# Two rows per token fetched from DRAM in place of scatter products, for six of eight expert pairs

## The chip, the cores and the metric

One core of a Trainium2 chip runs the whole program. The time is the device time of one execution in microseconds; what is compared is the median of several runs. The core has five engines with instruction queues of their own: TensorE (PE in the profile, its weight loads PEld), VectorE (DVE), ScalarE (ACT), GpSimd (POOL) and SyncE (SP), and sixteen DMA engines that all queues share.

## The reference, cut to what matters

Two transformer blocks run on 256 tokens of 1024 features in float32. The change lies in the last stage of the second block, a mixture of experts with 4 groups of 4 experts, of which each token takes two:

```python
def _hier_moe(h, w_r1, b_r1, w_r2, b_r2, w_gate, w_up, w_down):
    hf = h.reshape(B * T, D)                       # 256 x 1024
    g_logits = (hf @ w_r1 + b_r1)
    g_sel = jnp.argmax(g_logits, axis=-1)          # one group of four
    ...
    top_p, top_i = lax.top_k(e_prob, EXPERT_TOPK)  # two experts of the group
    expert_id = g_sel[:, None] * EXPERTS_PER_GROUP + top_i
    combine = jnp.sum(jax.nn.one_hot(expert_id, N_EXPERTS) * (g_w * top_p)[..., None], axis=1)
    hid = jax.nn.silu(jnp.einsum('nd,edf->nef', hf, w_gate)) * jnp.einsum('nd,edf->nef', hf, w_up)
    hid = hid * combine[..., None]
    out = jnp.einsum('nef,efd->nd', hid, w_down)   # w_gate, w_up 1024 x 256, w_down 256 x 1024 per expert

# block 2: x = x + merged @ w_out, then x = x + _hier_moe(rmsnorm(x), ...)
```

## The kernel before, in words

**The stage.** `moe` (from L1388) computes the router and, for every token and expert, the token's place among the tokens of that expert (`place`; `sel` marks the chosen ones). `experts` (from L1505) does the rest. Each expert has 64 slots (`SLOTS`), and the sixteen experts are handled as eight pairs (`NP`), so a pair is one tile of 128 slots: expert 0 of the pair in partitions 0 to 63, expert 1 in 64 to 127. Should an expert have more than 64 tokens, a loop behind the stage repeats it for the rest; it then runs with `table=None`, by the old way in both kernels.

**A pair's steps**, in the order in which TensorE meets them:
- its tokens' rows, transposed: for pairs 0 to 2 (`NEAR`) by products with a one-hot matrix (`gather`), for pairs 3 to 7 by an indirect DMA on GpSimd's queue (`fetch`, L1566) and eight transposes (`turn_rows`, L1574);
- `up` (L1622): 32 matmuls with the weights of gate and up, into one PSUM bank;
- `act_up` (L1630, L1631): Silu with the router's factor on ScalarE, the product on VectorE;
- `turn` (L1637): two transposes of the hidden rows, copied by ScalarE into `hf` (L1639); VectorE builds `pb`, the one-hot matrix slots x tokens, from `spread`;
- `down` (L1656): 16 matmuls with w_down into two PSUM banks of 128 slots x 512; each is split into two parts of fewer bits (`split_act`, L320 on ScalarE and a subtraction on VectorE);
- `back` (L1670): eight matmuls of `pb` with these parts give each token its rows' sum, in four pieces of 128 tokens x 512 columns; VectorE adds each piece to `y` in SBUF. `base` is what the stage adds to; for pair 0 it stands in place of `y`.

**The order.** `then(f, ...)` makes the instructions of `f` follow the last entry of `chain`, the list of the last matmul of each step, so that TensorE's order is the one written in the loop: up(p), turn(p - 1), turn_rows(p + 1), back(p - 2), down(p - 1). Pairs 6 and 7 are not added by `back`; at the end `finish` collects their products in PSUM piece by piece, adds `y` and stores the output from ScalarE's queue.

**`spread`** holds, for every pair, the places of all tokens, the same in 64 partitions: ScalarE copies them to SBUF, GpSimd's queue writes them to DRAM (L1530) and reads them back with a broadcast (L1532).

**The weights.** A pair has six pieces of 1 MB (four of up, two of down), each loaded by two DMAs of 512 KB on SyncE's queue (`load_part`, L278). Thirteen buffers form a ring (`get_raw`, `load`), and the next piece's DMA is issued when TensorE has read the buffer that it takes. DMAs from SyncE's and ScalarE's queues share eight semaphore counters in turn, and each waits for the DMA that had its counter before it.

Of the kernel before, what the change touches and what calls it, by code (L numbers as in the profile page):

```python
# [6 lines left out]
BF16 = mybir.dt.bfloat16  # L7
F32 = mybir.dt.float32
# [21 lines left out]
PRE = (1, 1, 1, 1, 2, 0, 0, 0)  # L30
WAIT = (17, 8)
SLOTS = 64
NEAR = 3

OFF1 = dict(q=0, k=1024, v=2048, g=3072, li=4096, lg=5120, ga=6144, gb=7168)
OFF2 = {}
# [117 lines left out]
CST["cb0"] = (CST["cb1"][0] + 128, 128)  # L154

_o = CST["rc"][0]
for _n, _w in (("slot", SLOTS), ("upper", 16), ("limit", 40), ("row", 1), ("token", 2)):
    CST[_n] = (_o, _w)
    _o += _w
NCST2 = _o - CST["rc"][0]  # L160
# [2 lines left out]
def _consts():  # L163
    c = np.zeros((P, NCST), np.float32)

    def put(name, v):
        o, w = CST[name]
        c[:, o:o + w] = v

    put("ident", np.eye(P))  # L170
    put("ones", np.ones((P, 128)))
    inv = np.float32(10000.0) ** (-np.arange(0, 128, 2, dtype=np.float32) / np.float32(128))
    ang = (np.arange(T1, dtype=np.float32)[None, :] * inv.astype(np.float32)[:, None]).astype(np.float32)
    cos, sin = np.cos(ang.astype(np.float64)), np.sin(ang.astype(np.float64))
    put("rc", np.concatenate([cos, cos], 0))
    put("rs", np.concatenate([sin, -sin], 0))
    i = np.arange(P)
    put("tri", i[None, :] >= i[:, None])
    lg = np.log(1.0 - 2.0 ** (-5.0 - np.arange(8)))
    kd = np.zeros((P, 3, 8))  # L180
    kd[:META, 0] = np.exp(-np.arange(META)[:, None] * lg[None]) * 128 ** -0.5
    kd[:, 1] = np.exp(-(META + i)[:, None] * lg[None]) * 128 ** -0.5
    kd[:, 2] = np.exp(-(META + P + i)[:, None] * lg[None]) * 128 ** -0.5
    put("kdec", kd.reshape(P, 24))
    qd = np.zeros((P, 2, 8))
    for t in range(2):
# [7 lines left out]
    put("row", 1 + np.arange(P)[:, None] % SLOTS)  # L194
    put("token", P * np.arange(2)[None, :] + np.arange(P)[:, None] - 2 * SEQ)
# [16 lines left out]
class _Build:  # L212
# [1175 lines left out]
    def moe(self, xt, xs, logits, sums, root, eps, sq, transposed, keep):  # L1388
# [97 lines left out]
        y = self.experts(xt, None, xs, tabs, place, table, count)  # L1486
        n = self.most
        with self.tc.If(n > SLOTS):

# [12 lines left out]
    def store(self, queue, y, t, c):  # L1502
        queue.dma_start(self.a["out"][t * P:t * P + P, c], y[:, t, c])

    def experts(self, base, y, xs, tab, place, table=None, count=None):  # L1505

        nc, v, act, te = self.nc, self.nc.vector, self.nc.scalar, self.nc.tensor
        ident = self.c("ident")
# [1 line left out]
        pl = self.bigt(F32R, (P, 2, NEXP * SLOTS))  # L1510
        chain = []
        if table:
            spread = self.cp.tile([P, 2, NP, P], BF16, name="spread", tag="spread")

        def slots(h):
            near = 2 * NEAR
            for t, e, n in ((0, 0, 4), (0, 4, near - 4), (1, 0, near)) if h == 0 else ((0, near, NEXP - near), (1, near, NEXP - near)):
                last = v.tensor_tensor(
                    pl[:, t, e * SLOTS:(e + n) * SLOTS].rearrange("p (e s) -> p e s", s=SLOTS),
                    self.c("slot").unsqueeze(1).to_broadcast([P, n, SLOTS]),  # L1520
                    place[:, 16 * t + e:16 * t + e + n].unsqueeze(2).to_broadcast([P, n, SLOTS]), op=ALU.is_equal)
            return last

        def places_spread():

            pt, rows = self.sp(), self.t(P, BF16)
            te.transpose(pt[:, 0:P], self.placep, ident)
            act.copy(rows[0:32, :], pt[0:32, 0:P])
            store = self.dram.tile([2, 2, NP, P], BF16, name=self.name("dram"), tag="places")
            nc.gpsimd.dma_start(store.rearrange("j t p n -> t p j n"), rows[0:32, :])  # L1530
            for j in range(2):
                nc.gpsimd.dma_start(spread[j * SLOTS:j * SLOTS + SLOTS, :, :, :].rearrange("s t p n -> s (t p n)"),  # L1532
                                    store[j].rearrange("t p n -> (t p n)").unsqueeze(0).to_broadcast([SLOTS, 2 * NP * P]))


        xg = {}
# [21 lines left out]
                    act.mul(dst, ps[:, 0:n], self.p("gffn", k))  # L1558
            chain.append(mm)

        ids = self.keep(NP, I32)
        far = {}

        def fetch(p):
# [16 lines left out]
        if table:  # L1581
            with self.tc.issue_after(last.ins):
                table()
                slots(1)
        else:
            slots(1)
        cw, cr, cc = self.s(8, tag="cw"), self.s(8, tag="cr"), self.t(160)

        def places():
# [21 lines left out]
        hid, back_, outs = {}, {}, {}  # L1611

        def up(p, ps=None, parts=range(4)):

# [19 lines left out]
        def turn(p):  # L1634
            th, pt = hid.pop(p), self.sp()
            for b in range(2):
                mm = te.transpose(pt[:, b * P:b * P + P], th[:, b * P:b * P + P], ident)  # L1637
            hf, pb = self.t(SEQ), self.t(SEQ, F32R)
            act.copy(hf, pt[:, 0:SEQ])  # L1639
            if table:  # L1640
                v.tensor_scalar(pb.rearrange("p (t n) -> p t n", t=2), spread[:, :, p, :], self.c("row"), None, op0=ALU.is_equal)
            else:
                for t in range(2):
                    mm = te.transpose(pt[:, SEQ + t * P:SEQ + t * P + P], pl[:, t, p * P:p * P + P].bitcast(F32), ident)
                v.tensor_copy(pb, pt[:, SEQ:512])
            chain.append(mm)
            hid[p], back_[p] = hf, pb

        def down(p, ws, bs, pool=None):

            hf = hid[p]
            pd = [self.mm() for _ in bs]
            for k in range(2):
                for b, ps in zip(bs, pd):
                    for j, w in enumerate(ws[k]):
                        mm = te.matmul(ps[j * SLOTS:j * SLOTS + SLOTS, :],  # L1656
                                       hf[:, k * P + j * SLOTS:k * P + j * SLOTS + SLOTS],
                                       w[:, b * 512:b * 512 + 512], start=k == 0, stop=k == 1)
            chain.append(mm)
            for b, ps in zip(bs, pd):  # L1660
                oh, ol = pool[b] if pool else [self.t(512, F32R) for _ in range(2)]
                self.split_act(oh, ol, ps)
                outs.setdefault(p, {})[b] = oh, ol
# [36 lines left out]
        early = ExitStack()  # L1700
        then(gather, 0, NEAR)
        for p in range(NP):
            if p == 1:
                ps = then(up, p, None, range(3))
                then(turn, 0)
                then(up, p, ps, range(3, 4))
            else:
                ps = then(up, p)
            if p == 0:
                then(places)  # L1710
            act_up(p, ps)
# [19 lines left out]
            if p > 1:  # L1731
# [4 lines left out]
        then(turn, NP - 1)  # L1736
# [4 lines left out]
        for p, ws, pool in pairs:  # L1741
            then(down, p, ws, (0,), pool)
        then(down, *pairs[0][:2], (1,), pairs[0][2])
# [82 lines left out]
```

## Time and profile before

| | |
|---|---|
| time, median of 3 runs | 1015.45 us (1015.33 to 1015.57) |
| the profiled execution's own time | 1015.9 us |
| its span in the trace | 1014.0 us |
| mean granted TensorE clock | 0.998 |
| VectorE, ScalarE, GpSimd busy | 758.2 (75%), 578.9 (57%), 45.5 (4%) us |
| DMA over the span | 205.95 MB, mean 203 GB/s |
| the last slices of 25.35 us each, GB/s | 271, 351, 400, 410, 411, 99 |

The span reaches from the first to the last record of the trace; the execution's own time has 1.9 us more around it. The profile page divides the span into 40 slices, and the last row of the table shows how much the DMA engines moved in the last six of them. The expert stage takes the last 100 us or so, four of these slices.

### The profile page before, as it was taken

Reading aid. Unit: us, or ns where it says so; the run is one execution under the profiler, and the core shown is the slowest. Engines: PE = TensorE matmul, PEld = TensorE weight load, DVE = VectorE, ACT = ScalarE, POOL = GpSimd, SP = SyncE. Lnnn points to the kernel's source line nnn. Section 1 sums busy time; section 2 is a strip of 40 time slices with the busy share of each in tenths; the row PEclk is TensorE's granted clock in tenths of the full one; section 3 lists DMA queues with packets and bytes.
Section 4 is the critical chain, followed back from the end, with each engine's and each line's share of the span. In section 5 each row is a group of like instructions: output and inputs, shape, how many; then the busy total and the mean of one; then the engine's idle time right before and its main releaser. Section 6 shows DMA issues by size and latency. Waiting matters only on the chain.

```text
span 1014.0 us, 16390 instructions
## 1 busy us (share of the span) xinstructions
PE 1005.6 (99%) x6101; PEld 847.8 (84%) x6101; DVE 758.2 (75%) x1472; ACT 578.9 (57%) x1119; POOL 45.5 (4%) x68
## 2 busy tenths in 40 slices
PE   9999999999999999999999999999999999999997
PEld 8999998888888888888889888888888898963443
DVE  6898987788888787777798767988857688553443
ACT  6678546575567666555667556776656665431111
POOL 1500000000000000000001000000010100020000
PEclk9999999999999999999999999999999999999999
DMA  9745564447556556556534653455555637799992
GB/s 349 234 146 188 167 190 155 136 124 248 186 171 194 186 187 187 175 187 199 175 111 148 210 183 121 133 191 166 170 181 183 208 125 269 271 351 400 410 411 99
DMA packets 59238, 205.95 MB, mean 203 GB/s; under 512 B 6973, under 2 KB 9165, under 8 KB 59024
## 3 DMA queue, kind: packets, MB, share of 16 engines
q1 hardware_dynamic: 56512, 200.34, 58.9%
q0 software_dynamic: 1200, 2.84, 0.8%
q10 hardware_dynamic: 1440, 1.66, 0.5%
q8 instruction: 50, 0.82, 0.3%
q14 instruction: 36, 0.29, 0.1%
HBM read 204.07 MB, written 2.11 MB: 203 GB/s over the span
## 4 chain that ended last, share of the span: by engine, by line
PE 98%; DVE 0%; ACT 0%; issue 0%; DVEq 0%; ACTq 0%
PE mm L374 57%; PE mm L1622 5%; PE mm L366 4%; PE mm L368 4%; PE mm L367 4%; PE mm L1656 3%; PE mm L415 2%; PE mm L417 2%; PE mm L416 2%; PE sp L1670 1%; PE sp L437 1%; PE mm L560 1%; PE mm L1552 1%; PE mm L553 0%; PE sp L1574 0%; PE sp L401 0%
## 5 line engine op out<-in xcount | busy, mean ns | idle before, releaser
L374 PE MATMUL mm<-big,hi 128*128 128x512 f32 x1664 | 586.5, 399 | 0.0
L374 PE MATMUL mm<-big,lo 128*128 128x256 f32 x1664 | 435.5, 281 | 0.0
L289 DVE TENSOR_TENSOR lo<-raw,hi 128x1024 fp32r<-128x1024 f32 (+1 forms) x279 | 338.2, 1214 | 57.9 <-ACT hi L288 53.0
L374 PEld LDWEIGHTS mm<-big,hi 128*128 128x128 f32 x1664 | 303.8, 188 | 58.1 <-issue 0.7
L288 ACT ACTIVATE hi<-raw 128x1024 fp32r<-128x1024 f32 (+1 forms) x279 | 293.8, 1054 | 96.9 <-PE mm L374 29.3
L374 PEld LDWEIGHTS mm<-big,lo 128*128 128x128 f32 x1664 | 313.0, 188 | 15.0 <-ACT big L323 0.6
L386 ACT COPY tmp<-mm 128x256 f32<-128x256 f32 x194 | 71.4, 368 | 129.9 <-PE mm L374 129.7
L387 DVE TENSOR_TENSOR tmp<-mm,tmp 128x256 f32<-128x256 f32 x194 | 81.3, 420 | 56.3 <-ACT tmp L386 56.1
L366 PE MATMUL mm<-big,hi 128*128 128x256 f32 (+1 forms) x360 | 103.4, 287 | 0.0
L368 PE MATMUL mm<-big,lo 128*128 128x256 f32 (+1 forms) x360 | 102.4, 284 | 0.0
L367 PE MATMUL mm<-big,hi 128*128 128x256 f32 (+1 forms) x360 | 102.3, 284 | 0.0
L367 PEld LDWEIGHTS mm<-big,hi 128*128 128x128 f32 x360 | 67.9, 189 | 0.1
L366 PEld LDWEIGHTS mm<-big,hi 128*128 128x128 f32 x360 | 67.9, 189 | 0.0
L368 PEld LDWEIGHTS mm<-big,lo 128*128 128x128 f32 x360 | 67.8, 188 | 0.0
L431 POOL TENSOR_TENSOR sml<-sml,keep 128x2 f32<-128x2 f32 (+4 forms) x17 | 18.6, 1095 | 663.6 <-DVE sml L892 184.2
L1631 DVE SCALAR_TENSOR_TENSOR tmp<-mm,sml,tmp 128x256 f32<-128x256 f32 x8 | 3.9, 484 | 36.5 <-ACT tmp L1630 36.5
L415 PE MATMUL mm<-hi,big 128*128 128x512 f32 (+1 forms) x80 | 30.0, 376 | 0.0
L417 PE MATMUL mm<-lo,big 128*128 128x512 f32 (+1 forms) x80 | 29.8, 372 | 0.0
L416 PE MATMUL mm<-hi,big 128*128 128x512 f32 (+1 forms) x80 | 29.7, 371 | 0.0
L1622 PE MATMUL mm<-big,big 128*64 128x512 f32 x128 | 28.4, 594 | 0.0
L320 ACT ACTIVATE tmp<-mm 128x512 fp32r<-128x512 f32 x14 | 8.4, 597 | 31.5 <-PE mm L1656 31.5
L1630 ACT ACTIVATE tmp<-mm,sml 128x256 f32<-128x256 f32 x8 | 3.8, 474 | 39.1 <-PE mm L1622 39.1
(427 smaller groups left out, 1208.2 us busy)
## 6 DMA issues: line engine op xcount, KB each, us to landing
raw<-w SPq DMA_DIRECT2D x288, 512.0 KB, 4.0
big<-w SPq DMA_DIRECT2D x36, 512.0 KB, 10.0
exp<-w SPq DMA_DIRECT2D x36, 512.0 KB, 10.2
raw<-w SPq DMA_DIRECT2D x16, 448.0 KB, 3.3
big<-xT SPq DMA_DIRECT2D x4, 272.0 KB, 3.7
big<-xT SPq DMA_DIRECT2D x1, 1024.0 KB, 8.0
big<-memT SPq DMA_DIRECT2D x1, 1024.0 KB, 5.4
dram<-big POOLq DMA_DIRECT2D x2, 512.0 KB, 5.5
```

Of the source, the lines that this page charges most:

```text
L288: nc.scalar.activation(hi[:, :n], raw[:, :n], AF.Copy)
L289: low = nc.vector.tensor_tensor(lo[:, :n], raw[:, :n], hi[:, :n].bitcast(F32), op=ALU.subtract)
L366: nc.tensor.matmul(out, wh, xh[:, k, cols], start=first, stop=False)
L367: nc.tensor.matmul(out, wh, xl[:, k, cols], start=False, stop=False)
L368: nc.tensor.matmul(out, wl, xh[:, k, cols], start=False, stop=last)
L374: nc.tensor.matmul(*args, start=first and args is both, stop=last and args is both)
L386: nc.scalar.copy(ps, both[:, n:2 * n])
L387: nc.vector.tensor_tensor(ps, both[:, 0:n], ps, op=ALU.add)
L415: nc.tensor.matmul(ps[:, :w], xh[:, k, c], wh, start=k == 0, stop=False)
L416: nc.tensor.matmul(ps[:, :w], xl[:, k, c], wh, start=False, stop=False)
L417: nc.tensor.matmul(ps[:, :w], xh[:, k, c], wl, start=False, stop=k == last)
L1622: mm = te.matmul(ps[j * SLOTS:j * SLOTS + SLOTS, :], x(k)[:, j * SLOTS:j * SLOTS + SLOTS], w[:, kc * 512:kc * 512 + 512], start=k == 0, st ...
```

## The change

For pairs 0 to 5 (`THROUGH = 6`) the scatter products go. `down` of such a pair copies its two PSUM banks to SBUF by ScalarE and writes them to a DRAM tile `sums3` of 768 rows x 1024, from ScalarE's queue, two DMAs of 128 x 512 (256 KB) each. `wanted` works out for each token which rows of `sums3` are its own: of the first twelve experts the token's two, by slot number, as the largest value and the rest of the sum; a token that has fewer gets an index out of bounds, and its row stays as it was. It is seven small VectorE operations, with two new constants. Once the last of the sums is written, four indirect DMAs on GpSimd's queue fetch these rows into two buffers `got` that were set to zero, 128 tokens each, and VectorE adds them to `base` and `y`. `spread` and `pb` remain for pairs 6 and 7 only. The diff, cut:

```diff
+NEAR, THROUGH = 3, 6
...
-            spread = self.cp.tile([P, 2, NP, P], BF16, name="spread", tag="spread")
+            spread = self.cp.tile([P, NP - THROUGH, 2, P], BF16, name="spread", tag="spread")
...
-            nc.gpsimd.dma_start(store.rearrange("j t p n -> t p j n"), rows[0:32, :])
+            for t in range(2):
+                nc.gpsimd.dma_start(store[:, :, t, :].rearrange("j p n -> p j n"), rows[16 * t:16 * t + 16, :])
...
+        def wanted():
+            val, b, two = self.t(32), self.t(32), self.s(4, tag="two")
+            v.scalar_tensor_tensor(val, place, float(SLOTS), sel.bitcast(F32), op0=ALU.is_le, op1=ALU.mult)
+            v.tensor_tensor(b, place, self.c("base"), op=ALU.add)
+            v.tensor_tensor(val, val, b, op=ALU.mult)
+            val = val.rearrange("p (t e) -> p t e", t=2)[:, :, 0:2 * THROUGH]
+            v.tensor_reduce(two[:, 0:2], val, axis=AX.X, op=ALU.max)
+            v.tensor_reduce(two[:, 2:4], val, axis=AX.X, op=ALU.add)
+            v.tensor_tensor(two[:, 2:4], two[:, 2:4], two[:, 0:2], op=ALU.subtract)
+            v.tensor_scalar(wants, two, -1.0, None, op0=ALU.add)
...
+        # down
+            if table and p < THROUGH:
+                for b, ps in zip(bs, pd):
+                    orow = self.t(512)
+                    act.copy(orow, ps)
+                    nc.scalar.dma_start(self.sums3[p * P:p * P + P, b * 512:b * 512 + 512], orow)
+                return
...
         for p in range(NP):
-            if p == 1:
+            if p == 1 or table and p == NP - 1:
                 ps = then(up, p, None, range(3))
-                then(turn, 0)
+                then(turn, p - 1)
                 then(up, p, ps, range(3, 4))
...
-            act_up(p, ps)
+            if not 1 < p < NP - 1:
+                act_up(p, ps)
...
+            if 1 < p < NP - 1:
+                with self.tc.issue_after(held[0].ins):    # after turn's copy of hf
+                    act_up(p, ps)
...
-            if p > 1:
+            if p > 1 and not table:
                 then(back, p - 2, y)
             if 0 < p < NP - 1:
                 then(down, p - 1, weights(p - 1), (0, 1))
+            if table and p == THROUGH - 1:
+                got = [self.bigt(shape=(P, 2, D)) for _ in range(2)]
+                for g in got:
+                    nc.gpsimd.memset(g, 0.0)
+            if table and p == THROUGH:
+                for t in range(2):
+                    for i, g in enumerate(got):
+                        nc.gpsimd.indirect_dma_start(
+                            g[:, t, :], None, self.sums3[:, :],
+                            bass.IndirectOffsetOnAxis(wants[:, 2 * i + t:2 * i + t + 1].bitcast(mybir.dt.uint32), 0),
+                            bounds_check=THROUGH * P - 1, oob_is_err=False)
+                        v.tensor_tensor(y[:, t, :], g[:, t, :], (y if i else base)[:, t, :], op=ALU.add)
```

At the end the order becomes first half of down(6), turn(7), second half of down(6), first half of down(7), then `finish`, the second half of down(7), and `finish` again.

**Where TensorE's instructions stand: the end of pair 7's up.** Before, the last four matmuls of up(7) (line 1622), the transposes of pair 6's hidden rows, then the eight of `back` for pair 5 (1670), and the transposes of pair 7:

```order
L1622 MATMUL mm_10869<-big_10718,big_10285 64x512 x4
L1637 MATMUL sp_10889<-keep_91,tmp_10813 128x128 x2
L1670 MATMUL sp_10896<-tmp_10861,tmp_10820 128x512
L1670 MATMUL sp_10896<-tmp_10862,tmp_10820 128x512
L1670 MATMUL sp_10900<-tmp_10861,tmp_10820 128x512
L1670 MATMUL sp_10900<-tmp_10862,tmp_10820 128x512
L1670 MATMUL sp_10904<-tmp_10865,tmp_10820 128x512
L1670 MATMUL sp_10904<-tmp_10866,tmp_10820 128x512
L1670 MATMUL sp_10908<-tmp_10865,tmp_10820 128x512
L1670 MATMUL sp_10908<-tmp_10866,tmp_10820 128x512
L1637 MATMUL sp_10912<-keep_91,tmp_10886 128x128 x2
```

In the changed kernel (up 1642, turn 1657, down 1677):

```order
L1642 MATMUL mm_10804<-big_10664,big_10298 64x512 x4
L1657 MATMUL sp_10817<-keep_91,tmp_10757 128x128 x2
L1642 MATMUL mm_10804<-big_10671,big_10298 64x512 x4
L1677 MATMUL mm_10832<-big_10699,tmp_10820 64x512 x2
L1677 MATMUL mm_10832<-raw_10702,tmp_10820 64x512
L1677 MATMUL mm_10832<-raw_10704,tmp_10820 64x512
L1657 MATMUL sp_10841<-keep_91,tmp_10828 128x128 x2
```

The eight products are gone, pair 6 is turned ahead of the last quarter of up(7), and pair 7 behind the first half of down(6).

**Where ScalarE's instructions stand: around down(4).** Before: the Silu of one pair (line 1630), the copy of the turned hidden rows of the pair ahead of it (1639), and the first parts of the split of that pair's sums (320):

```order
L1630 ACTIVATE tmp_10725<-mm_10695,sml_10167 128x256
L1639 COPY tmp_10731<-sp_10728 128x256
L320 ACTIVATE tmp_10780<-mm_10770 128x512
L320 ACTIVATE tmp_10784<-mm_10771 128x512
L1630 ACTIVATE tmp_10813<-mm_10788,sml_10167 128x256
```

In the changed kernel (hidden rows' copy 1659, Silu 1650, sums' copies 1684, their stores 1685), with the counters that each waits for; DMAHW is one of the eight that the DMAs share:

```order
L1659 COPY tmp_10681<-sp_10678 128x256 [waits PE_49]
L1650 ACTIVATE tmp_10684<-mm_10648,sml_10179 128x256 [waits DMASW3_49,DMASW2_49]
L1684 COPY tmp_10716<-mm_10706 128x512 [waits DMAHW5_49,PE_49]
L1685 DMA dram_10177<-tmp_10716 128x512 [waits DMAHW0_49,Activation_49]
L1684 COPY tmp_10719<-mm_10707 128x512 [waits DMAHW7_49,PE_49]
L1685 DMA dram_10177<-tmp_10719 128x512 [waits DMAHW2_49,Activation_49]
L1659 COPY tmp_10754<-sp_10751 128x256 [waits PE_49]
```

The copy of the hidden rows now precedes the Silu, and each sum's copy is followed by a DMA issue that waits for a counter; the next pair's copy of hidden rows stands behind both.

## Rows read from the trace of the kernel before

**Rows 1.** Page, part 1: busy us (share of the span) x instructions, by engine.

```profile
PE 1005.6 (99%) x6101; PEld 847.8 (84%) x6101; DVE 758.2 (75%) x1472; ACT 578.9 (57%) x1119; POOL 45.5 (4%) x68
```

**Rows 2.** Chain of waits in order of time, 912 to 1014: start, length, work.

```profile
959.53 6.87 PE mm L1622 x32
966.39 0.37 PE sp L1637 x2
966.76 0.87 PE sp L1574 x8
967.64 1.85 PE sp L1670 x8
969.49 3.58 PE mm L1656 x16
973.07 6.87 PE mm L1622 x32
...
995.91 5.30 PE mm L1656 x24
1001.22 2.05 PE sp L1670 x8
1003.27 1.87 PE mm L1656 x8
1005.14 1.96 PE sp L1670 x10
```

**Rows 3.** Engines by stretch: length, busy (x) each, PEclk, DMA share, GB/s.

```profile
904.50:918.50 14.00, 14.00 (x74) 5.77 (x72) 1.98 (x7) 3.26 (x6) 3.15 (x4) 1.00 1.03 351
...
926.00:963.00 37.00, 37.00 (x184) 16.23 (x184) 17.13 (x30) 5.75 (x12) 2.97 (x3) 1.00 1.03 409
963.00:990.00 27.00, 27.00 (x134) 11.64 (x132) 11.42 (x20) 3.86 (x8) 0.00 (x0) 1.00 1.03 411
990.00:994.00 4.00, 4.00 (x22) 1.43 (x19) 0.00 (x0) 0.47 (x2) 0.00 (x0) 1.00 0.52 208
```

**Rows 4.** Last weight DMA: issue (timeline of SP); landing (DMA issues, 984.2 to 985).

```profile
984.26 0.33 SPq L278 DMA_DIRECT2D raw<-w  x1
...
raw<-w SPq DMA_DIRECT2D x1, 512.0 KB, 10.0
```

**Rows 5.** DMA queues and issues, 1003 to 1007, the first two output stores.

```profile
q10 hardware_dynamic: 288, 0.52, 35.5%
...
out<-big ACTq DMA_DIRECT2D x2, 256.0 KB, 2.1
```

**Rows 6.** DMA queues and issues, 926 to 963, three gathers of token rows.

```profile
q0 software_dynamic: 432, 0.72, 5.2%
...
big<-dram,keep POOLq DMA_INDIRECT x3, 7.5
```

**Rows 7.** DMA queues and issues, 895 to 899, token rows written beside weights.

```profile
DMA packets 450, 1.66 MB, mean 416 GB/s; under 512 B 47, under 2 KB 47, under 8 KB 449
...
q0 software_dynamic: 214, 0.82, 50.5%
...
big<-w SPq DMA_DIRECT2D x1, 512.0 KB, 3.8
```

**Rows 8.** DMA issues from 913.2 to 913.3, one weight DMA behind `spread`.

```profile
raw<-w SPq DMA_DIRECT2D x1, 512.0 KB, 5.2
```

**Rows 9.** Engines by stretch after the last matmuls, columns as in rows 3.

```profile
1007.30:1010.50 3.20, 0.02 (x1) 0.00 (x0) 1.18 (x3) 0.00 (x0) 0.00 (x0) 1.00 0.31 105
1010.50:1014.00 3.50, 0.00 (x0) 0.00 (x0) 0.00 (x0) 0.00 (x0) 0.00 (x0) 0.51 0.23 70
```

**Rows 10.** Groups by line, 918 to 995 (last row: whole span): busy, mean, idle.

```profile
L320 ACT ACTIVATE tmp<-mm 128x512 fp32r<-128x512 f32 x12 | 7.2, 597 | 28.9 <-PE mm L1656 28.9
...
L1639 ACT COPY tmp<-sp 128x256 f32<-128x256 f32 x6 | 2.2, 365 | 0.1
...
L289 DVE TENSOR_TENSOR lo<-raw,hi 128x1024 fp32r<-128x1024 f32 x263 | 320.8, 1222 | 51.8 <-ACT hi L288 46.8
```

More of the change, by code (lines that the diff above doesn't have):

```diff
@@ L32 @@
 SLOTS = 64
-NEAR = 3
+NEAR, THROUGH = 3, 6
 OFF1 = dict(q=0, k=1024, v=2048, g=3072, li=4096, lg=5120, ga=6144, gb=7168)
@@ L156 @@
 _o = CST["rc"][0]
-for _n, _w in (("slot", SLOTS), ("upper", 16), ("limit", 40), ("row", 1), ("token", 2)):
+for _n, _w in (("slot", SLOTS), ("upper", 16), ("limit", 40), ("row", 1), ("token", 2), ("base", 32), ("place", NEXP // 2)):
     CST[_n] = (_o, _w)
@@ L194, in _consts @@
     put("row", 1 + np.arange(P)[:, None] % SLOTS)
+    put("base", SLOTS * (np.arange(32) % NEXP)[None, :])
+    put("place", P * np.arange(NEXP // 2)[None, :] + np.arange(P)[:, None])
     put("token", P * np.arange(2)[None, :] + np.arange(P)[:, None] - 2 * SEQ)
@@ L1484, in table @@
             self.split_act(tabs[:, :, 0, :], tabs[:, :, 1, :], tab)
-        y = self.experts(xt, None, xs, tabs, place, table, count)
+        y = self.experts(xt, None, xs, tabs, place, table, count, sel)
         n = self.most
@@ L1503, in store, with experts @@
         queue.dma_start(self.a["out"][t * P:t * P + P, c], y[:, t, c])
-    def experts(self, base, y, xs, tab, place, table=None, count=None):
+    def experts(self, base, y, xs, tab, place, table=None, count=None, sel=None):
         nc, v, act, te = self.nc, self.nc.vector, self.nc.scalar, self.nc.tensor
@@ L1528, in places_spread @@
             act.copy(rows[0:32, :], pt[0:32, 0:P])
-            store = self.dram.tile([2, 2, NP, P], BF16, name=self.name("dram"), tag="places")
-            nc.gpsimd.dma_start(store.rearrange("j t p n -> t p j n"), rows[0:32, :])
+            store = self.dram.tile([2, NP, 2, P], BF16, name=self.name("dram"), tag="places")
+            for t in range(2):
+                nc.gpsimd.dma_start(store[:, :, t, :].rearrange("j p n -> p j n"), rows[16 * t:16 * t + 16, :])
             for j in range(2):
-                nc.gpsimd.dma_start(spread[j * SLOTS:j * SLOTS + SLOTS, :, :, :].rearrange("s t p n -> s (t p n)"),
-                                    store[j].rearrange("t p n -> (t p n)").unsqueeze(0).to_broadcast([SLOTS, 2 * NP * P]))
+                nc.gpsimd.dma_start(spread[j * SLOTS:j * SLOTS + SLOTS, :, :, :].rearrange("s p t n -> s (p t n)"),
+                                    store[j, THROUGH:NP].rearrange("p t n -> (p t n)").unsqueeze(0).to_broadcast([SLOTS, 2 * (NP - THROUGH) * P]))
         xg = {}
@@ L1559, in gather @@
             chain.append(mm)
-        ids = self.keep(NP, I32)
+        ids, wants = self.keep(NP, I32), self.keep(4, I32)
+        def wanted():
[8 more added lines that the diff above has]
+            v.tensor_scalar(wants, two, -1.0, None, op0=ALU.add)
         far = {}
@@ L1586, in experts @@
             slots(1)
+        if table:
+            wanted()
+            self.sums3 = self.dram.tile([THROUGH * P, D], F32, name=self.name("dram"), tag="sums")
         cw, cr, cc = self.s(8, tag="cw"), self.s(8, tag="cr"), self.t(160)
@@ L1609, in places @@
             v.tensor_tensor(cr, pw4[:, :, 0, 16], cc[:, 0:144].rearrange("p (a e) -> p a e", a=8)[:, :, 16], op=ALU.add)
-        hid, back_, outs = {}, {}, {}
+        hid, back_, outs, held = {}, {}, {}, {}
         def up(p, ps=None, parts=range(4)):
@@ L1638, in turn @@
             hf, pb = self.t(SEQ), self.t(SEQ, F32R)
-            act.copy(hf, pt[:, 0:SEQ])
+            held[0] = act.copy(hf, pt[:, 0:SEQ])
             if table:
-                v.tensor_scalar(pb.rearrange("p (t n) -> p t n", t=2), spread[:, :, p, :], self.c("row"), None, op0=ALU.is_equal)
+                if p >= THROUGH:
+                    v.tensor_scalar(pb.rearrange("p (t n) -> p t n", t=2), spread[:, p - THROUGH, :, :], self.c("row"), None, op0=ALU.is_equal)
             else:
@@ L1710, in experts @@
                 then(places)
-            act_up(p, ps)
+            if not 1 < p < NP - 1:
+                act_up(p, ps)
+            turned = p == 1 or table and p == NP - 1
             if p == 2 and y is None:
@@ L1718, in experts @@
                         early.enter_context(self.tc.issue_after(i.ins))
-            if p > 1:
+            if p and not turned:
                 then(turn, p - 1)
+            if 1 < p < NP - 1:
+                with self.tc.issue_after(held[0].ins):
+                    act_up(p, ps)
             if table:
@@ L1730, in experts @@
             early.close()
-            if p > 1:
+            if p > 1 and not table:
                 then(back, p - 2, y)
@@ L1734, in experts @@
                 then(down, p - 1, weights(p - 1), (0, 1))
-        then(turn, NP - 1)
+            if table and p == THROUGH - 1:
[10 more added lines that the diff above has]
+                        v.tensor_tensor(y[:, t, :], g[:, t, :], (y if i else base)[:, t, :], op=ALU.add)
+        if not table:
+            then(turn, NP - 1)
         last = self.bigt(F32R, (P, 4, 512))
@@ L1740, in experts @@
         first, second = [(NP - 2, 0), (NP - 2, 1)], [(NP - 1, 0), (NP - 1, 1)]
-        for p, ws, pool in pairs:
-            then(down, p, ws, (0,), pool)
-        then(down, *pairs[0][:2], (1,), pairs[0][2])
+        then(down, *pairs[0][:2], (0,), pairs[0][2])
+        if table:
+            then(turn, NP - 1)
+            then(down, *pairs[0][:2], (1,), pairs[0][2])
+        then(down, *pairs[1][:2], (0,), pairs[1][2])
+        if not table:
+            then(down, *pairs[0][:2], (1,), pairs[0][2])
         finish(y, self.PIECES[:2], first + second)
```

## The prediction

> **What bounds the kernel now.** I read four views in this order. The page's busy table first: TensorE works 1005.6 us of a span of 1014.0 [rows 1], so at first sight whatever leaves TensorE leaves the time. Then the chain of waits in order of time, over the expert stage [rows 2]. A pair of experts costs 13.54 us there, from 959.53 to 973.07: up 6.87, turn 0.37, the turned rows of a later pair 0.87, back 1.85, down 3.58, and no idle piece stands between them. Third, the busy time of every engine by stretch [rows 3], for the column that the first two views do not have: from 926 to 990 the DMA engines show a share of 1.03 (over 1, since their records overlap a little) at 409 to 411 GB/s, and they fall quiet only after 990. This is a second resource with no room. A weight DMA of 512 KB takes 0.524 MB / 0.410 = 1.28 us of it, so the twelve of a pair take 15.3 us, 1.8 more than TensorE needs for a pair: the stage lives on a lead that was fetched earlier and shrinks. Fourth, the last weight DMA by itself: issued at 984.26, landed 10.0 us later [rows 4], that is at 994.3. Its first reader is the 13th of the 24 matmuls that begin at 995.91 [rows 2], at 995.91 + 12 x 0.221 = 998.6. What is left of the lead at the end is 4.3 us.
>
> **The change part by part.** *Removed from TensorE:* `back` of pairs 0 to 5, eight matmuls each, six pieces of 1.85 us in the chain [rows 2]: 6 x 1.85 = 11.1 us, all on today's path. If the weights were always there, the span would be 1014.0 - 11.1 = 1002.9.
>
> *Moved on TensorE and ScalarE:* without `back`, hf of a pair must be ready after the 0.87 us of turned rows alone. It is now copied before the Silu; the copy takes 0.365 [rows 10] and fits, and pair 6, which has no turned rows behind it, is turned inside up(7) with a quarter of it (1.72 us) as cover. Cost 0. If that cover were short, down would start a few tenths late. *ScalarE and VectorE:* the two copies out of PSUM per pair cost ScalarE what its half of the split cost, 0.597 each [rows 10]; the two DMA issues per pair stand behind them in its queue, and ScalarE is busy 5.75 of 37 us [rows 3]. VectorE loses four adds and two subtractions per pair. The eight small operations of `wanted` and `places_spread`'s second DMA fall where VectorE is busy 1.98 of 14 us [rows 3]. All at 0. Each store also shares one of eight counters with weight DMAs and waits for the one that had it before; ScalarE then holds the next hf. I take 0, because that weight was issued several DMAs earlier and TensorE will be waiting for later weights anyway; the other end is a few us of waiting on ScalarE that the same DMA wait covers.
>
> *Added to the DMA engines,* the part that decides. Every byte that moves before the last weight delays it, since there is no idle share between 926 and 990.
> - Twelve stores of 256 KB (128 rows of 2 KB). The nearest row is the output stores, the same shape on the same queue: two of them take 35.5% of 4.0 us = 1.42 us of all sixteen engines [rows 5], twelve 8.5, and 8.3 after dividing by the 1.03. Lower end 3.15 MB at 409 GB/s = 7.7, upper 8.5. All twelve precede the last weight: the last leaves between 977.4 (where down(5) ends now, 973.07 + 13.54 = 986.6, less 5 x 1.85) and 986.6. That loads and stores share one rate is seen where the token rows are written to DRAM beside weights: half the share each, 416 GB/s for both together [rows 7].
> - Four gathers. The reference's own routing sends 388 of 512 (token, expert) choices to the first twelve experts, so 388 rows of 4 KB, 1.59 MB. Three fetches of the same kind moved 0.72 MB in 5.2% of 37 us = 1.92 us [rows 6]; 1.59 MB takes 4.25, and 4.1 after the 1.03. Lower end 3.9 (409 GB/s). They start once the last store has landed (2.1 us after its issue [rows 5]) and land some 7.5 us after theirs [rows 6], also before the last weight.
> - `spread` shrinks from 512 to 128 KB. In the stretch of the old one, 904.5 to 918.5, the engines moved 351 GB/s instead of 409 [rows 3]: 14.0 - 4.91/0.409 = 2.0 us lost, and with its own 1.3 us it cost 3.3; three quarters are 2.5. But the weight DMA behind it is issued only at 913.2 to 913.3, when TensorE frees its buffer, and lands 5.2 us later [rows 8]; a lone one needs 3.8 [rows 7]. So at most 1.4 comes forward. I take -1.4, with 0 and -2.5 as ends.
>
> *The sum.* The last weight lands at 994.3 + 8.3 + 4.1 - 1.4 = 1005.3. TensorE alone could read it by about 988, so DMA sets the end. Behind the landing come two matmuls of down(7) 0.44, the first product pieces 2.1, the second half of down(7) 1.87, the last pieces 1.96, and what now follows the last matmul, 1014.0 - 1007.1 = 6.9 [rows 2]: 13.3 us. Span 1018.6, 4.6 more than now. The profiled execution took 1015.9 for its span of 1014.0, so I expect 1020.5 for such a one; it lies 0.45 above the median of 1015.45, hence **1020.0** as the time. The ends of the terms give 9.1 to 12.8 instead of 11.0, so 1018.1 to 1021.9. The change loses if it puts more than 1014.0 - 13.3 - 994.3 = 6.4 us before the last weight. Where the stall goes: the lead of 4.3 turns into some 18 us of waiting in sum (11.1 that TensorE comes earlier and 11.0 that the weights come later), from pair 5 or 6 on. The four VectorE adds (1.222 each [rows 10]) end before the last split needs VectorE.
>
> The Trainium skill, "DMA: Bandwidth & Descriptors", section Specifications, puts the fabric's ceiling for the sixteen engines at 435 GB/s; by it the stores would be an estimated 7.2 us and the sum 1.1 us less. The trace stays at 409 to 416, so the rows' price stands.
>
> **The rivals.**
> (a) *Stores ride along.* Stores read SBUF and weights write it; if an engine moves one while it moves the other, the twelve cost the weights nothing. Then 4.1 - 1.4 = 2.7 us are added, below the 6.4 that decide, and the span is 994.3 + 2.7 + 13.3 = 1010.3: 3.7 faster, 1011.7. Against it: the halved shares in [rows 7]. For it: that row is a stretch of 4 us, and for half of it no weights were queued. This is the other side, and the point is stores at under 3.7 us. Chance 0.11.
> (b) *TensorE stays the bound*, as the busy table suggests, with weights arriving in time all the same: 1015.45 - 11.1 + 0.3 = 1004.6. It needs the engines to carry more than 411 GB/s, which no stretch after 926 shows. Chance 0.04.
> (c) *The clock falls.* TensorE would work about two thirds of the time from pair 6 on. After its last matmul at 1007.3 the granted clock is still 1.00 until 1010.5 and then 0.51, the lower level of 1.2 GHz [rows 9]; before that it never waited in this stage, so the trace does not say what short waits do. If the 6.4 us of matmuls behind the last weight ran at the lower level throughout, 6.4 more: 1026.4; for half of them, 1023.2, which I take. Chance 0.14. The Trainium skill, "TensorE: Matmul & The Clock Gate", section HAM oscillation, tells of a kernel whose matmuls came in bursts between DMA waits and began each at the low clock; by that rule (c) is the case.
> (d) *Smaller on every term*, or weights that regain part of it in a bubble of today's stream (the 351 GB/s stretch): 6.4 to 8.4 us added, no difference that can be told, about 1016. Chance 0.09.
>
> **How the numbers follow.** The forecast, weights late by 9 to 13 us and the clock held, has 0.62. A difference of 0.2% (2.0 us) is about what a measurement of this kernel can tell from none. Faster is (a) and (b): 0.15. Same, 1013.4 to 1017.5, is (d): 0.09. Slower is the forecast and (c): 0.76. The range takes in the forecast's own 1018.1 to 1021.9, (d), and most of (c): 1013.5 to 1025.0; it leaves out (a), (b) and the worst of (c), 0.19 together.
>
> **What would show it.** Right: up to about pair 4 a pair takes 11.7 us on TensorE without waits; from pair 5 or 6 on, idle time before the matmuls of up and down, ended by weight DMAs; the DMA share 1.0 until past 1003 and the last weight landing near 1005; 13 us from there to the end. The stores' queue should show about 0.7 us of all engines per store. Wrong: a last weight before 1000 (a), no waits on TensorE (b), a granted clock under 1.0 before the last matmul (c), or waits of TensorE that end on ScalarE or VectorE, which I have put at nothing.

## The result, and the profile after

| | before | after |
|---|---|---|
| time, median of 6 runs each | 1015.53 us (1015.33 to 1019.02) | 1023.57 us (1022.27 to 1025.91) |
| ratio after to before | | 1.0076, 95% interval 1.0056 to 1.0095 |
| the profiled execution's own time, its span | 1015.9, 1014.0 us | 1023.4, 1021.6 us |
| mean granted TensorE clock | 0.998 | 0.998 |

The change makes the kernel 8 us slower; 4.6 were forecast, and the time lies inside the range of 1013.5 to 1025.0. Two of the six runs (1025.82 and 1025.91) had a mean clock of 0.996 and 0.995 and were 2.1 to 3.6 us longer than the other four; they have no trace, so where in the program their clock fell is open.

In this document L is the time from the first matmul of down(0) to the last packet of the weights' DMA queue, worked out from each profile's records; it leaves out where the expert stage begins. L was 78.5 us before and is 90.3 now. (The expectations of e1 to e4 count it by the chain, from 916.81 to the landing at 1007.33, which gives 90.5 and 78.8, some 0.25 more; the later ones count it as here.)

The busy table of the page, which answers to [rows 1], looks as if nothing had happened, though 48 matmul records of 0.23 us are gone:

```profile
PE 1006.0 (98%) x6053; PEld 841.3 (82%) x6053; DVE 740.0 (72%) x1441; ACT 578.8 (57%) x1119; POOL 53.6 (5%) x75
```

The chain of waits in order of time (start, length, work) is the view that shows it. Up, turned hidden rows, turned rows, down now stand as L1642, L1657, L1591, L1677, the products of `finish` as L1697:

```profile
916.81 3.43 PE mm L1677 x16
...
931.94 6.87 PE mm L1642 x32
938.81 0.37 PE sp L1657 x2
939.18 0.87 PE sp L1591 x8
940.05 3.58 PE mm L1677 x16
943.64 6.87 PE mm L1642 x32
...
966.85 6.08 DMA dram<-tmp
...
973.41 7.67 DMA exp<-w
...
981.10 8.25 DMA big<-w
...
993.93 13.40 DMA raw<-w
...
1007.38 1.07 PE mm L1677 x2
1008.45 2.14 PE sp L1697 x8
1010.59 1.87 PE mm L1677 x8
1012.46 1.96 PE sp L1697 x10
```

A pair takes 943.64 - 931.94 = 11.70 us without a wait, 1.84 less than in [rows 2]; that part of the plan works. From 966 on the chain runs through DMAs: one store of sums, then weights to the last one, which lands at 1007.33. The engines by stretch (columns as in [rows 3]) show why they are late:

```profile
926.00:945.00 19.00, 19.00 (x98) 7.43 (x96) 3.36 (x6) 3.83 (x8) 1.98 (x2) 1.00 1.03 416
...
985.00:990.00 5.00, 4.02 (x16) 1.12 (x15) 0.00 (x0) 0.00 (x0) 0.00 (x0) 1.00 1.02 404
990.00:995.00 5.00, 4.91 (x18) 1.20 (x14) 0.03 (x1) 0.85 (x2) 1.98 (x2) 1.00 0.93 330
995.00:1000.00 5.00, 3.59 (x10) 0.85 (x12) 0.46 (x1) 0.33 (x1) 1.98 (x2) 1.00 1.01 394
1000.00:1005.00 5.00, 3.79 (x12) 0.88 (x12) 3.05 (x3) 1.12 (x3) 0.00 (x0) 1.00 1.02 411
1005.00:1010.00 5.00, 3.69 (x11) 1.57 (x12) 4.01 (x5) 0.60 (x1) 0.00 (x0) 1.00 0.19 76
```

The DMA share stays near 1 until 1005, ten to fifteen us longer than before, at 394 to 416 GB/s; the granted clock stays at 1.00 throughout. One stretch, 990 to 995, has a share of 0.93 and carries only 330 GB/s.

TensorE's waits from 963 on, as the profile lists them (us in total, times, longest), add up to 5.8:

```profile
PE mm L1677 <- DMA raw<-w: 3.9, 5, 1.2
PE mm L1642 <- DMA big<-w: 1.0, 2, 0.8
PE mm L1642 <- DMA exp<-w: 0.9, 2, 0.7
```

TensorE's last piece ends 7.3 later than before (1014.42 against 1007.10). Take off 1.3 for a later start of the stage and add the 11.1 that were removed: 17.1 us of waiting. By this sum the other 11.3 sit inside busy time. TensorE's timeline (start, busy, group, idle before it) shows where:

```profile
997.26 1.07 PE L1677 MATMUL mm<-raw,tmp 128*64 128x512 f32 x2 [1.17 <-DMA raw<-w]
...
999.93 1.08 PE L1677 MATMUL mm<-big,tmp 128*64 128x512 f32 x4
```

A matmul of down stands in the trace as two records. Two records, the matmul of one expert, take 1.07 us; four, the matmuls of both experts of a pair, take 1.08: they have 64 columns each and run side by side, their records beginning within 0.01 us of each other. When the second expert's weights land a DMA later than the first's, they run one after the other, and TensorE counts as busy all the while.

### The profile page after: what moved, and what is told of

Same layout as the page of the kernel before. It is cut to its first block, busy times and chain, and to the rows that moved or that the text cites. A ratio compares the mean times of both kernels' runs of the same rounds, so it can differ in the third digit from the quotient of the medians.

```text
span 1021.6 us, 16313 instructions
## 1 busy us (share of the span) xinstructions
PE 1006.0 (98%) x6053; PEld 841.3 (82%) x6053; DVE 740.0 (72%) x1441; ACT 578.8 (57%) x1119; POOL 53.6 (5%) x75
## 4 chain that ended last, share of the span: by engine, by line
PE 93%; DMA 4%; DVE 1%; ACT 0%; issue 0%; SPq 0%; DVEq 0%; ACTq 0%
PE mm L377 57%; PE mm L369 4%; PE mm L371 4%; PE mm L370 4%; PE mm L1642 4%; PE mm L1677 2%; DMA raw<-w 2%; PE mm L418 2%; PE mm L420 2%; PE mm L419 2%; PE sp L440 1%; DMA big<-w 1%; DMA exp<-w 1%; DMA dram<-tmp 1%; PE mm L1556 1%; PE sp L404 0%
## 5 line engine op out<-in xcount | busy, mean ns | idle before, releaser
L1592 DVE TENSOR_TENSOR big<-sp,keep 128x512 f32<-128x512 f32 x10 | 6.9, 686 | 54.2 <-PE sp L1591 54.2
L1642 PE MATMUL mm<-big,big 128*64 128x512 f32 x128 | 31.3, 597 | 1.0 <-DMA big<-w 1.0
L1659 ACT COPY tmp<-sp 128x256 f32<-128x256 f32 x8 | 3.0, 372 | 47.8 <-PE sp L1657 47.8
L419 PE MATMUL mm<-hi,big 128*128 128x512 f32 (+1 forms) x80 | 29.7, 372 | 0.0
L1642 PE MATMUL mm<-exp,big 128*64 128x512 f32 x96 | 25.4, 597 | 1.1 <-DMA exp<-w 0.9
```

The source lines that it names most:

```text
L419: nc.tensor.matmul(ps[:, :w], xl[:, k, c], wh, start=False, stop=False)
L1642: mm = te.matmul(ps[j * SLOTS:j * SLOTS + SLOTS, :], x(k)[:, j * SLOTS:j * SLOTS + SLOTS], w[:, kc * 512:kc * 512 + 512], start=k == 0, st ...
```

## The experiments

The time of each is a median beside runs of before on the same chip; the ratio is to those. These medians of before lie between 1015.5 and 1016.4 us, so two times of the table can differ by up to 0.9 for that alone.

| run | time, us | ratio to before, 95% interval | L, us |
|---|---|---|---|
| before | 1015.5 | | 78.5 |
| the change | 1023.6 | 1.0076 (1.0056 to 1.0095) | 90.3 |
| e1 stores from GpSimd's queue | 1022.9 | 1.0060 (1.0042 to 1.0078) | 89.9 |
| e2 half width | 1021.6 | 1.0039 (1.0022 to 1.0055) | 88.9 |
| e9 half width, GpSimd's queue | 1016.7 | 1.0010 (1.0001 to 1.0019) | 85.0 |
| e3 no fetch | 1019.4 | 1.0026 (1.0014 to 1.0037) | 86.9 |
| e4 no stores, no fetch | 1011.1 | 0.9936 (0.9919 to 0.9953) | 78.5 |
| e5 before, without back | 1011.8 | 0.9958 (0.9943 to 0.9973) | 78.0 |
| e6 before, with stores | 1022.2 | 1.0060 (1.0044 to 1.0075) | 88.1 |
| e7 two pairs through DRAM | 1022.8 | 1.0066 (1.0052 to 1.0080) | 83.1 |
| e10 the same, adds late | 1019.8 | 1.0046 (1.0030 to 1.0062) | 82.6 |
| e11 one pair, adds late | 1021.1 | 1.0056 (1.0037 to 1.0075) | 80.9 |
| e12 one pair, adds in between | 1016.6 | 1.0011 (1.0002 to 1.0020) | 80.7 |
| e13 two pairs, adds in between | 1016.0 | 0.9998 (0.9989 to 1.0007) | 83.4 |

### The bytes: e3, e4, e5, e6

e3 leaves out the fetch, e4 the stores as well:

```diff
-                        nc.gpsimd.indirect_dma_start(g[:, t, :], None, self.sums3[:, :], ...)
...
-                    nc.scalar.dma_start(self.sums3[p * P:p * P + P, b * 512:b * 512 + 512], orow)
```

> The four indirect fetches of sums are left out (the two buffers stay zero, so the result lacks the sums of pairs 0 to 5); the stores stay. Theory (bytes): the last weight lands 4.1 us earlier (86.4 after down(0) begins) and the time falls by 4. Rival 1 (shared counters): the fetches are not on these counters; nothing changes before them, and the last weight comes under 1 us earlier. Rival 3 (fetches land beside or behind the last weights, since they are issued at 992.6 to 996.5 and the last weight at 993.9): 1 to 2 us.

> Stores and fetches both left out (result lacks the sums of pairs 0 to 5); ScalarE's copies, the smaller spread and the new order stay. Theory (bytes): the last weight lands about 12.4 us earlier (78.1 after down(0) begins; 78.8 before the change), and the time falls by 12 to about 1011, still later than TensorE alone would need (1004 to 1006), because the weights themselves are what DMA has no room for. Rival 4 (TensorE bound once the added transfers go): 1004 to 1006.

L fell by 3.4 without the fetch (4.1 expected), and by another 8.3 without the stores; then it is what it was before the change, to 0.1, and the time is 12.5 below the changed kernel's (13.4 if each is taken against its own runs of before), where the theory had 12. TensorE is not the bound even then: 1011.1 is 6.5 above the 1004.6 that it would need by the forecast.

e4 also answers for `spread`, whose smaller size is still in it: nothing came of it. In the stretch of [rows 3] in which the old one was read, e4 shows

```profile
904.50:918.50 14.00, 14.00 (x74) 5.65 (x72) 1.68 (x7) 2.88 (x5) 3.21 (x4) 1.00 0.97 341
```

341 GB/s for 351. The DMA share is 0.97 there instead of 1.03, so the engines now carry less: argued, not tried, the weights already issued come sooner and the next have to wait until TensorE frees a buffer.

e5 takes only the products away from the kernel before, e6 only adds twelve stores to it:

```diff
-            if p > 1:
+            if p > 1 and not table:
                 then(back, p - 2, y)
+            elif p == 2:
+                v.tensor_copy(y, base)
```

> The kernel before with the scatter products and adds of pairs 0 to 5 left out (their sums are missing from the result), nothing added. Theory (the weights' own stream has no room): the last weight still lands 78.5 us after down(0) begins, so of the 11.1 us that leave TensorE only the lead of 4.3 and little more is gained: 4 to 5 us less than before, 1010.5 to 1011.5. Rival 4 (TensorE bound, the DMA engines follow): 11 less, 1004.5.

```diff
                 outs.setdefault(p, {})[b] = oh, ol
+                if table and p < 6:
+                    nc.scalar.dma_start(self.sums3[p * P:p * P + P, b * 512:b * 512 + 512], oh.bitcast(F32))
```

> The kernel before with twelve added stores of 256 KB from ScalarE's queue (the first part of each split of pairs 0 to 5, to a DRAM tile that nobody reads), nothing removed. Theory (bytes): the last weight lands 8.3 us later, 86.9 after down(0) begins; the lead of 4.3 is used up, and the time grows by 4 (8.3 - 4.3). Rival (stores ride along with loads on other paths): 78.5 still, and no change of time.

e5 gained 4.2 us of the 11.1 taken away, with L within 0.5 of before: the weights are the floor, and the busy table's 99% was not the whole bound. e6 lost 6.3 where 4 were expected: L grew by 9.5, not 8.3, with stretches such as

```profile
996.00:1002.00 6.00, 4.65 (x14) 1.19 (x13) 2.34 (x5) 0.97 (x2) 0.00 (x0) 1.00 0.91 341
```

so that something besides bytes holds weights up where stores stand among them. SyncE's queue, which issues the weights, waited 26.1 us for the stores in e6, and by itself e6 cannot tell bytes from such waits. Stores that ride along with loads would have left L alone here and, with the waits gone, in e1 below; there L is 89.9, and that rival is out.

### The counters: e1, e2, e9

In the changed kernel SyncE's queue, which issues the weights, waited for the stores, by its list of waits from 925 to 1005 (us in total, times, longest):

```profile
SPq L281 <- DMA dram<-tmp: 26.0, 10, 5.7
```

A weight DMA waits for the DMA that had its counter before it, eight back in the joint order of both queues; where that is a store, the weight cannot be issued before down has run, been copied, stored and landed. SyncE's queue waited before the change as well, 40.7 us in the same stretch for other weights; so the 26.0 us are not a loss by themselves, and it takes a run to price them.

```diff
-                    nc.scalar.dma_start(self.sums3[...], orow)
+                    nc.gpsimd.dma_start(self.sums3[...], orow)
```

> The twelve stores of sums are issued from GpSimd's queue instead of ScalarE's, so they no longer share the eight counters with the weight DMAs; bytes and everything else as in the changed kernel. Theory (bytes on DMA engines that have no room): the last weight lands 90.5 us after down(0) begins, as in the changed kernel (1007.33 - 916.81), within 1 us, and the time stays within 1 us of it. Rival 1 (weight DMAs held back on the shared counters: SyncE's queue waited 26.0 us for stores): the last weight comes 2 us or more earlier, up to 8, and the time falls by as much. Rival 2 (ScalarE held up by its store issues): TensorE's waits on ScalarE go, under 1 us.

The wait is gone, and L hardly moves (89.9 for 90.3). The dip is filled, as the stretch 970 to 1000 shows, first of the changed kernel, then of e1:

```profile
970.00:1000.00 30.00, 26.57 (x94) 8.15 (x92) 2.42 (x5) 3.00 (x7) 3.96 (x4) 1.00 1.01 394
```

```profile
970.00:1000.00 30.00, 26.75 (x94) 8.28 (x92) 2.92 (x6) 3.30 (x8) 8.72 (x8) 1.00 1.03 411
```

The bytes alone then hold L nearly where it was.

e2 halves the width of sums and fetched rows, with the stores on ScalarE's queue; e9 is e2 with the edit of e1:

```diff
-            self.sums3 = self.dram.tile([THROUGH * P, D], F32, ...)
+            self.sums3 = self.dram.tile([THROUGH * P, D // 2], F32, ...)
...
-                    nc.scalar.dma_start(self.sums3[p * P:p * P + P, b * 512:b * 512 + 512], orow)
+                    nc.scalar.dma_start(self.sums3[p * P:p * P + P, b * 256:b * 256 + 256], orow[:, 0:256])
...
-                            g[:, t, :], None, self.sums3[:, :],
+                            g[:, t, 0:D // 2], None, self.sums3[:, :],
```

> The sums are stored and fetched at half width: the twelve stores have 128 KB instead of 256, the four fetches rows of 2 KB instead of 4, the number of DMAs and their order stay; half of each token's sums is left out of the result. Theory (bytes): half of the stores' 8.3 and of the gathers' 4.1 us go, the last weight lands 6.2 us earlier (84.3 after down(0) begins), and the time falls by 6. Rival 1 (shared counters): a store still has to be issued and to land before the weight DMA that has its counter; it lands perhaps 1 us sooner, and the time falls by under 2.

> Half-width stores and fetches as in the run before (half of each token's sums is left out of the result), with the stores issued from GpSimd's queue, so that they share no counter with the weights. Theory now (both bounds stand beside each other: bytes, and the store-to-weight wait, which took over when only the bytes were halved): with both eased the DMA engines stay at 400 to 410 GB/s until the last weight, which lands 33.4 MB / 0.400 = 83.5 to 84.5 us after down(0) begins instead of 88.9, and the time falls 5 to 6 us below the changed kernel's. Rival (neither bytes nor counters: TensorE's own order of reading holds the last buffers): 88 to 89 again, and 1 to 2 us.

e2 came out as the rival had it: L fell by 1.4, not 6.2, and SyncE's queue waited 29.7 us for the stores. e9 settles it: with the counters apart as well, no wait for a store is left, L falls by 5.3 (to 85.0, where 83.5 to 84.5 were expected) and the time by 6.9. The stretch 955 to 990, first of e2, then of e9:

```profile
955.00:990.00 35.00, 32.50 (x140) 11.23 (x136) 3.62 (x7) 4.43 (x9) 1.80 (x1) 1.00 0.97 370
```

```profile
955.00:990.00 35.00, 33.49 (x149) 12.26 (x146) 3.62 (x7) 4.62 (x10) 8.69 (x10) 1.00 1.03 411
```

370 GB/s with the counters shared, 411 without. As far as these runs tell, two bounds stand within 1.4 us of each other in the changed kernel, bytes first and the store-to-weight wait right behind; relieving one alone shows little.

### Fewer pairs: e7, e10 to e13

With the lead of 4.3 us, one or two pairs through DRAM should pay. All five have back for the remaining pairs:

```diff
-NEAR, THROUGH = 3, 6
+NEAR, THROUGH = 3, 2
...
-            if p > 1 and not table:
+            if p > 1 and (not table or p - 2 >= THROUGH):
                 then(back, p - 2, y)
```

> The changed kernel with pairs 0 and 1 through DRAM only and pairs 2 to 7 by products (THROUGH = 2, back for pairs 2 to 5). Theory: TensorE saves 2 x 1.85 = 3.7; four stores cost 2.6 to 2.8 and the fetch of 136 rows (0.56 MB) 1.4, so the last weight lands 82.5 to 82.8 after down(0) begins, and with the changed kernel's 14.3 behind it the span is 915.4 + 82.7 + 14.3 = 1012.4, 1 to 2 us below before. Rival 1 (stores held against weights by the counters throughout): the same as before or slower.

L came close to the expected 82.5 to 82.8 (83.1), the time did not. The chain shows a piece that no weight causes (issue: the engine waited for nothing that the profile shows):

```profile
928.37 0.60 DVE big L1592
928.97 17.67 issue
946.64 0.42 DVE big L1779
947.06 0.72 issue
947.78 0.35 DVE tmp L1662
948.13 0.61 DVE big L1592
948.74 0.04 issue
948.78 9.90 PE mm L1642 x32
```

The adds of the fetched rows (L1779) stood in VectorE's queue ahead of the next pair's turned rows (L1592) and waited for the fetch, which waited for the stores; TensorE stood idle for 5.8 us behind them. After that the up took 9.90 us, not 6.87: the granted clock (the column before the DMA share) had fallen to its lower level, 1.2 GHz. The idling and the lower clock cost 8.8 us together, where 3.7 were to be saved.

```profile
946.00:949.00 3.00, 0.22 (x2) 0.22 (x4) 2.36 (x4) 0.00 (x0) 0.09 (x1) 0.78 1.04 398
949.00:952.00 3.00, 3.00 (x8) 0.79 (x8) 2.48 (x3) 0.00 (x0) 0.00 (x0) 0.50 1.04 400
952.00:955.00 3.00, 3.00 (x10) 0.85 (x8) 2.68 (x4) 0.00 (x0) 0.00 (x0) 0.59 1.03 407
```

e10 moves the buffers, the fetches and the adds beside pairs 5 and 6, and e11 does the same with one pair:

```diff
-            if table and p == THROUGH - 1:
+            if table and p == 5:
...
-            if table and p == THROUGH:
+            if table and p == 6:
...
-                        v.tensor_tensor(y[:, t, :], g[:, t, :], (y if i else base)[:, t, :], op=ALU.add)
+                        v.tensor_tensor(y[:, t, :], g[:, t, :], y[:, t, :], op=ALU.add)
```

> THROUGH = 2 as in the run before, but the zeroed buffers, the fetches and VectorE's adds of the fetched rows stand where the changed kernel has them (beside pairs 5 and 6) instead of beside pair 2, so that VectorE does not wait for the fetch ahead of the next pair's turned rows. Theory: the 17.7 us piece and the lower clock of the run before go; the last weight stays at about 83.2 after down(0) begins, the last matmul ends at 83.2 + 7.2 = 90.4 after it (92.0 before the change), so the time is 1 to 2 us below before. TensorE alone would give 88.3 and 3.7 below. Rival (the wait of VectorE was only moved): 3 us or more slower than before.

> The same with THROUGH = 1: one pair through DRAM, its fetch and adds beside pairs 5 and 6. Theory: TensorE saves 1.85 (last matmul 90.2 after down(0) begins); two stores 1.3 and the fetch of 71 rows 0.7 put the last weight at 80.5 to 81.2, and 7.2 behind it is 88.4 at most, so TensorE is the bound and the time is 1.5 to 2 us below before. Rival (one pair's saving is lost in waits as well): same as before.

Both lost again, 4.0 and 5.3 us against their runs of before: the scheduler put the adds among back's adds of pair 5, and TensorE's transposes of pair 7 waited for those. The same row stands in both profiles' waits; e10's:

```profile
PE sp L1657 <- DVE big L1705: 3.2, 1, 3.2
```

In e10 the clock fell to 0.50 at 1001.3, 1.3 us after this wait ended, for 3.4 us; in e11, behind a wait as long, it held. The stretch 1000 to 1010, first of e10, then of e11:

```profile
1000.00:1010.00 10.00, 9.97 (x35) 3.75 (x36) 5.83 (x9) 1.70 (x4) 0.00 (x0) 0.83 0.07 26
```

```profile
1000.00:1010.00 10.00, 9.39 (x43) 4.35 (x43) 6.94 (x11) 2.17 (x4) 0.00 (x0) 1.00 0.15 54
```

It cost e10 1.7 us: the 16 records of down behind the transposes took 5.28 there and 3.58 in e11.

In e12 and e13 they stand one pair earlier (`p == 4` and `p == 5` in the diff above), where VectorE had been idle.

> THROUGH = 1 as in the run before, with the zeroed buffers beside pair 4 and the fetches and VectorE's adds beside pair 5, where VectorE was idle from 974 to 980, instead of at the end of pair 6. Theory: the 3.2 us for which the transposes of pair 7 waited behind those adds go, the last matmul ends 90.2 after down(0) begins (92.0 before the change), and the time is 1.5 to 2 us below before. Rival (VectorE's adds, or the memory they take from the weights' ring, are in the way wherever they stand): 2 us or more slower than before.

> The same with THROUGH = 2. Theory: the last weight lands 82.6 to 83.2 after down(0) begins, as in the two runs with THROUGH = 2; if the matmuls behind it take 7.2, the last one ends at 90.3, so the time is 1 to 2 us below before, no better than with one pair: here the weights are the bound. TensorE alone would give 88.3 and 3.7 below. Rival as above: 2 us or more slower than before.

The wait behind the adds is gone, since neither profile lists a wait of TensorE after 880, yet nothing is won: e12 is 0.1% slower, e13 equal to before. In e12's chain a pair with back takes 13.76 us instead of 13.54, as its eight products mostly take 2.07 or so instead of the 1.85 of [rows 2],

```profile
966.71 2.07 PE sp L1697 x8
```

in four pairs, and the new order at the end takes 0.8 more; of the 1.85 saved 0.2 is left. What makes these pieces longer in the new order was not tried. In e13 the weights are late again at the very end: its last 16 records of down take 4.59 us for 3.58, as busy time, and of the 1.7 us expected of the stage (the last matmul at 90.3 after down(0) begins for 92.0) 0.7 is left (91.3). No version that computes the whole result beat the kernel before.

## Why the prediction was right, and where it was not

**What bounds the kernel.** Right: DMA, not the 99% of TensorE. Shown by e5 (4.2 us gained for 11.1 removed) and e4 (L back to 78.5 with the transfers gone). Rival (b), TensorE as the bound, is out by the same runs. That stores take their share of one rate was read from [rows 7], which does not show it: there the weights' queue has 99.6% of the engines from 895 to 897 and the other queue 97.4% from 897 to 899, one behind the other. It is the changed kernel that shows it, below.

**Stores, 8.3.** Right: L differs by 8.3 between e3 and e4. The queues of weights (q1) and stores (q10) in the changed kernel from 930 to 990 (packets, MB, share of the sixteen engines), at 412 GB/s for all together:

```profile
q1 hardware_dynamic: 5875, 21.38, 88.3%
q10 hardware_dynamic: 1397, 2.56, 11.1%
```

The stores took 6.7 us for 2.56 MB, 0.68 per store, where 0.7 was forecast. In e3 the stores share the counters too, so its 8.3 is not bytes alone; with the counters apart, stores and fetch cost 11.4 together (e1 against e4) and 6.4 at half width (e9), by the forecast's prices 12.4 and 6.2. Rival (a) fell with e6 and e1.

**Fetch, 4.1.** The engines' time for it was right, 20.2% of the 20 us from 990 to 1010, 4.0 us:

```profile
q0 software_dynamic: 576, 1.59, 20.2%
```

L paid 3.4 (change against e3). From 990 to 996 the engines move 337 GB/s with the fetch and 316 without, so a part of it falls into a dip that stands empty in e3; that this is all of the difference is not shown.

**Spread, -1.4.** Wrong: 0.0 (e4 against before; e5, which keeps the large `spread` and has no back either, lies 0.5 lower still). The step that failed is the reading of [rows 3] and [rows 8]: the low 351 GB/s was put down to `spread` alone, but with it smaller the engines moved no more in the same stretch (341). That they were short of issued weights is argued. The low end of 0 was the value. (`wanted` has seven operations, not the eight of the prediction; nothing hangs on it.)

**The counters, "all at 0".** Wrong in its mechanism: it had ScalarE held behind weights, while SyncE's weights were held behind stores, 26.0 us in all; ScalarE itself waited once for a counter, 0.5 us. In the change itself it costs little, since the bytes hold the weights almost as long: L falls by 0.4 in e1. It is why halving the bytes alone gains 1.4 us and with the counters apart 5.3.

**The sum.** 78.5 + 8.3 + 3.4 = 90.2, against 90.3 measured; the forecast's 11.0 became 11.7. That these are so close is in part luck: a fetch 0.7 too dear stands against a `spread` 1.4 too hopeful. Two smaller sums were off. Behind the last landing come 1021.6 - 1007.3 = 14.3, not 13.3: the last weight's matmuls cost 1.07, not 0.44, as nothing runs beside them, and the rest is spread over the products and the last stores. And down(0) began 1.3 later in the execution profiled (916.81 for 915.47). Most of this is chance of the execution: TensorE's 101st matmul record, far ahead of the stage, already begins 1.0 later (20.59 us into the span for 19.61; at 19.61 in e11, which has the same program there). The other 0.3 is not explained. In the thirteen profiles beside that of before the stage begins 0.4 to 2.3 later. 1018.6 + 0.7 + 1.0 + 1.3 = 1021.6. The median missed by 0.6 more, since the profiled execution lies 0.2 below it and that of before lay 0.45 above.

**The waits.** 18 us were forecast, 17.1 came, from the up of pair 6 on, but only a third of them as idle time; "idle time before the matmuls" was too simple a test.

**The clock, rival (c).** Not in the profile: 1.00 until after the last matmul, with waits of up to 1.2 us. In e7 it fell behind a gap of 5.8 us. The Trainium skill, "TensorE: Matmul & The Clock Gate", section HAM oscillation, tells of matmuls that began at the low clock behind each of their DMA waits, and the prediction took (c) to follow from it; but the waits told of there are longer than any of the change, whose trace therefore does not test it, and e7 agrees with it (0.50 behind the gap). Behind waits of 3.2 us the clock fell in e10 and held in e11. Nor does every fall have a gap before it: the profiles of e10 and e13 show 0.50 for 3.4 us from 527, in an earlier stage, with TensorE busy without a pause from 520 on. So it is not shown that the wait caused the fall in e10.

**Fetched adds on VectorE, "end before the last split".** Just so: the last one began at 1007.16 for 1.23 us, and no matmul waited. e7, e10 and e11 show what happens where TensorE does wait for such adds.

## What to carry to other kernels

Before trading matmuls for DRAM traffic, read the DMA share of the stage beside the busy table: where both are full, the gain is capped by the lead that the loads have (here 4.3 us), and every byte that moves before the last load is paid at the full rate. Where stores and loads share counters in turn, a store that depends on late compute holds loads behind it; give it a queue with counters of its own, and test bytes and waits together, as either one alone hides the other. An add that waits for a fetch belongs where nothing in its queue is needed next.

## What was not expected of the hardware

One 64-column matmul of down alone cost as much as the two of a pair side by side (1.07 against 1.08 us), so that waiting for weights shows up as busy time. After an idle gap of 5.8 us in e7 the granted clock was 0.50 from 949 to 952 and 1.00 from 955 on, and an up of 6.87 us took 9.90; gaps of 1.2 us in the changed kernel left it at 1.00, one of 3.2 us was followed by 0.50 for 3.4 us in e10 and by 1.00 in e11.
